# One set of activation tiles, overwritten in halves, for all stages of the first two blocks of a hybrid decoder step

## The chip, the cores and the metric

The kernel runs on one core of one Trainium2 chip. The metric is the device time of one execution in microseconds. TensorE does the matmuls, VectorE and ScalarE the elementwise work, GpSimd (POOL in the profile) a part of it, and SyncE (SP) issues the DMAs. Each engine works through its own queue in order.

## What is computed

One decoder layer over a prompt of 2048 tokens and 8 x 8 sample tokens, width 1024, in float32:

```python
mix = jnp.concatenate([oa, ob, oc, od], axis=-1).astype(dt) @ prm['w_out'][li]
h = h + mix

gu = rmsnorm(h, prm['norm2_g'][li]) @ prm['w_ffn_in'][li]
h = h + (jax.nn.silu(gu[..., :D_FF]) * gu[..., D_FF:]) @ prm['w_ffn_out'][li]

gate = jax.nn.sigmoid(rmsnorm(h, prm['ple_norm_g'][li]) @ prm['w_ple_gate'][li])
h = h + (pl @ prm['w_ple'][li]) * gate
```

Ahead of that stands an RMSNorm, a projection `w_in` and four token mixers (a to d), whose outputs are `oa` to `od`; behind it a last RMSNorm gives `y_prompt`. D_FF is 2816.

## The kernel before

The prompt is cut into four blocks of 512 tokens, each of four row tiles of 128 tokens. First `in_proj` runs for all blocks (to about 885 us); then, for each block, the part after the mixers: `rest(0)`, `rest(1)`, `rest(2)`, and `rest7(3)` for the last block with the sample rows. The mixers of a block run between and beside these stages: `mixers(b)` and `rest(b)` are written one after the other, and a scheduler orders all instructions by priority (`S.at(...)`, the table `PRIO`) and by when it expects operands to be ready. `S.at(0)` puts an instruction ahead of everything that is ready.

Matmuls of float32 are made of three passes: every operand is split into a high part, cast by ScalarE (`split` line 306, scaled 309, weights line 290), and a low part, the difference, on VectorE (307, 310) or for half of the weights on GpSimd (293). An activation tile `act` holds 128 of the 1024 features for all 512 tokens, high and low; `act8` (line 231) takes eight of them from a pool of eight in the stages after the mixers. The passes are hi x hi, hi x lo, lo x hi.

`rest` (line 511) works so. `mixed` (line 646) loads the four mixer outputs, 128 x 1024 each (line 657), and splits them into eight act tiles. Four residual tiles `h` of 128 x 1024 are loaded from x_prompt (`load_x`, line 388, DMA issue at line 391) into a pool of five buffers. `out_mm` (line 444) multiplies by w_out: four columns of 256, and in each column four row tiles; one row tile and column is 24 matmuls into one PSUM bank (`mm_a`, matmuls at line 374), and `add` (line 520) adds it to `h`. The matmuls of blocks 0 and 1 share three PSUM banks; from `rest(2)` on there are six.

The second norm needs all of a row of `h`. `Norm.prep` takes the reciprocal root (`rstd`, lines 323 to 335) and scales the rows into an `xs` tile (line 68); `Norm.step` transposes one feature tile of two row tiles on TensorE (line 85) and splits it into an act tile. With one pool of act tiles the norm's tiles come from the same eight buffers as those of the output projection, so its steps are written after all of w_out. Only block 2 has a second pool (`act2`) and hands the norm to `out_mm`, which calls `prep` and `step` as soon as row tiles have their last column.

Then the feed-forward part (`mm_b`, matmuls at line 354; w_ffn_out again through `out_mm` with columns of 512), the ple norm, and `per_layer_out`: four quarters of gate (w_ple_gate, 24 matmuls) and up (w_ple, 6 matmuls) for every row tile, lines 592 to 594. After the last quarter `finish(i)` (line 578) scales row tile i and stores it to y_prompt (line 579); the `h` buffer is free when the store has read it.

Here and in the prediction C is the boundary of blocks 0 and 1, B the second norm of block 0 and D that of block 1. A line after the change is the line before plus 1 near line 85 to 510, and plus 2 or 1 in `rest`: 307 is 308, 374 is 375, 391 is 392, 520 is 522, 578 is 579.

Of the kernel before, what the change touches and what calls it, by code (L numbers as in the profile page):

```python
# [11 lines left out]
F32 = mybir.dt.float32  # L12
# [9 lines left out]
D = 1024  # L22
T = 2048
TB = 512
NB = T // TB
NS = 64
TBS = TB + NS
# [9 lines left out]
class Norm:  # L37
# [1 line left out]

    def __init__(self, S, src, gain, groups, scale=True, ahead=True):
        self.S, self.src, self.gain, self.groups, self.scale, self.ahead = S, src, gain, groups, scale, ahead
        self.acts, self.rows, self.ready, self.r = S.act8(TBS if (4,) in groups else TB), {}, {}, {}
        self.last, self.done, self.fresh = groups[-1][-1], set(), True
        self.of = {i: g[-1] for g in groups for i in g}
        self.it = self.steps()
        if ahead:
            with S.at(0):
                self.rows = {i: src(i) for i in [i for g in groups for i in g][:4]}  # L50
# [142 lines left out]
class Step:  # L193
# [314 lines left out]
            self.split(pas[k], ps[:, k * NS:(k + 1) * NS])  # L508
        return pa, pas

    def rest(self, b, mix, smix):

        nc, I, O = self.nc, self.I, self.O
        with_s = smix is not None
        tiles = [i for i, _ in self.tiles(with_s)]
        h = {}

        def add(i, c, ps):
            d = h[i][:, c]
            nc.vector.tensor_tensor(d, ps, d, op=ALU.add)  # L520

        acts = self.mixed(mix, smix)
        nt = TBS if with_s else TB
        for i in tiles:
            h[i] = self.load_x(self.hp.tile([128, D], F32, name="h"), b, i)
        norm2 = lambda **k: self.norm(lambda i: (h[i], False), self.gain["norm2_g"], with_s, **k)

        norm = norm2(ahead=False) if len(self.actps) > 1 else None
        self.out_mm(acts, I["w_out"][0], KT, 256, with_s, add, norm)
        norm = norm or norm2()  # L530
        wi, wo = I["w_ffn_in"][0], I["w_ffn_out"][0]
        KC = 3
        f0 = 0
        while f0 < FT:
            n = KC if f0 else FT % KC
            gs = []
            if f0 + n == FT:
                pa, pas = self.per_layer(b, with_s)
            for f in range(f0, f0 + n):
                us = [self.units([wi[:, c0:c0 + 128]], KT, 4) for c0 in (f * 128, D_FF + f * 128)]  # L540
                if f:
                    ps = [self.mm_b(u, acts, KT, with_s) for u in us]
                else:

                    acts, w0 = norm.upto(1), TB // 2
                    t = self.bank()
                    ps = [[(0, w0, self.mm_piece(t[:, j * w0:(j + 1) * w0], u, acts, KT, 0))] for j, u in enumerate(us)]
                    norm.all()
                    for p, u in zip(ps, us):
                        t = self.bank()[:, :nt - w0]  # L550
                        p.append((w0, nt - w0, self.mm_piece(t, u, acts, KT, w0)))
                g = self.gp.tile([128, 2, TBS], F32R, name="g", tag="g")
                gs.append(g)
                for (t, m, gate), (_, _, up) in zip(*ps):
                    th = self.ev.tile([128, TBS], F32, name="ev")[:, :m]
                    nc.scalar.activation(th, gate, AF.Tanh, scale=0.5)
                    nc.vector.scalar_tensor_tensor(th, th, 1.0, gate, op0=ALU.add, op1=ALU.mult)
                    nc.vector.scalar_tensor_tensor(th, th, 0.5, up, op0=ALU.mult, op1=ALU.mult)
                    self.split(g[:, :, t:t + m], th)
            w = wo[f0 * 128:(f0 + n) * 128]  # L560
            f0 += n
            if f0 < FT:
                self.out_mm(gs, w, n, 512, with_s, add)
        norm = self.norm(lambda i: (h[i], False), self.gain["ple_norm_g"], with_s, scale=False, ahead=False)
        self.out_mm(gs, w, n, 512, with_s, add, norm, True)
        self.per_layer_out(b, h, norm, pa, pas)

# [75 lines left out]
                self.out_mm(*last, 512, with_s, add, norm, True, mid=with_s)  # L643
                self.per_layer_out(b, h, norm, pa, pas)

    def mixed(self, mix, smix):

        nc = self.nc
        with_s = smix is not None
        acts = self.act8(TBS if with_s else TB)  # L650
        if with_s:
            ms = self.ev.tile([128, TBS], F32, name="ev")[:, :KT * NS].rearrange("p (k n) -> p k n", k=KT)
# [2 lines left out]
        for j in range(4):  # L655
            m = self.xsp.tile([128, D], F32, name="xs").rearrange("p (k n) -> p k n", k=2)
# [1421 lines left out]
def step_kernel(ctx, tc, I, O):  # L2078
    nc = tc.nc
    S = Step(ctx, nc, tc, I, O)  # L2080
# [10 lines left out]
    mix = [m for _, m in zm]  # L2091
# [35 lines left out]
    with S.working("p", 16):  # L2127
        norm = S.in_proj(0, z[0], None, S.norm1(0, False), (1, True))
# [3 lines left out]
        norm = S.in_proj(2, z[2], None, norm, (3, False))  # L2132
        mixers(1)
        S.in_proj(3, z[3], None, norm)
    with S.working("f", 8, 3, 5):
        S.rest(0, mix[0], None)
        mixers(2)
        S.rest(1, mix[1], None)
        mixers(3)
        M.banks.close()  # L2140
        sample_mixers()
        with S.tc.tile_pool(name="act2", bufs=KT, reuse_waits="tile") as p:
            S.actps, S.nacts = [p] + S.actps, 0
            with S.more():
                S.rest(2, mix[2], None)
# [21 lines left out]
```

## Time and profile before

| | before |
|---|---|
| median of 3 runs | 3416.94 us (3409.40 to 3417.16) |
| the profiled execution | 3413.59 us, span 3411.8 us |
| TensorE busy | 3304.8 us, 97% of the span |
| TensorE weight loads | 82% |
| VectorE, ScalarE, GpSimd busy | 61%, 39%, 22% |
| mean granted TensorE clock | 0.982 |

Times are microseconds from the start of the span. A row of a timeline is: start, duration, engine and line, operation, output <- inputs, shape, how many; in brackets the idle time of the engine ahead of it and what ended it. SPq rows are the issues of DMAs on SyncE's queue. Matmuls overlap in the pipeline, so a row's duration is longer than the distance to the next.

### The profile page before, as it was taken

To read this page: it belongs to the slowest core of one execution; us is meant where nothing else is said; L and a number is where in the kernel's file an instruction comes from. 1 tells how busy PE (TensorE), PEld (TensorE's weight loads), DVE (VectorE), ACT (ScalarE), POOL (GpSimd) and SP (SyncE) were. 2 spreads that over 40 slices of the span, in tenths; PEclk is the share of its full clock that TensorE was granted. 3 is DMA by queue.
4 is the path that set the end of the run, shared out by engine and by line. 5 is a ranking of instruction groups with operands and counts; after the bars stand their busy time and mean duration, and the time that the engine had idled before them with its cause. 6 is when DMAs were issued, how large, how long until landed. Compare 5 with 4: busy or idle time off the path is not lost. (4 is left out here: it accounts for less than half of the span.)

```text
span 3411.8 us, 64337 instructions
## 1 busy us (share of the span) xinstructions
PE 3304.8 (97%) x23998; PEld 2784.0 (82%) x23998; DVE 2067.0 (61%) x5691; ACT 1322.2 (39%) x2753; POOL 756.4 (22%) x656
## 2 busy tenths in 40 slices
PE   7999999999999999998999999999999999999998
PEld 6788987878887778788878777788777789889888
DVE  4455566654577756588876457754332466877765
ACT  4433445323344223355333335344233244434343
POOL 2212112122112122112112212131121222334321
PEclk9999999999999999999999999999999999999999
DMA  7645445544433333444333443344544543223222
GB/s 211 185 121 146 128 119 157 153 126 146 128 106 104 98 91 112 116 115 129 114 98 105 121 113 106 108 137 135 148 138 121 156 145 121 63 81 93 77 89 69
DMA packets 621756, 411.78 MB, mean 121 GB/s; under 512 B 155357, under 2 KB 572876, under 8 KB 621444
## 3 DMA queue, kind: packets, MB, share of 16 engines
q1 hardware_dynamic: 618184, 405.12, 41.1%
q8 instruction: 189, 3.10, 0.4%
q10 hardware_dynamic: 3260, 2.55, 0.3%
q14 instruction: 123, 1.01, 0.1%
HBM read 348.77 MB, written 61.18 MB: 120 GB/s over the span
## 5 line engine op out<-in xcount | busy, mean ns | idle before, releaser
L354 PE MATMUL mmp<-act,whi 128*128 128x512 f32 (+1 forms) x3616 | 1108.0, 386 | 6.6 <-ACT ev L378 4.3
L293 POOL TENSOR_TENSOR wlo<-wraw,whi 128x512 fp32r<-128x512 f32 (+1 forms) x400 | 557.9, 1397 | 2055.0 <-ACT whi L290 1314.6
L290 ACT CAST whi<-wraw 128x512 fp32r<-128x512 f32 (+1 forms) x800 | 491.6, 619 | 840.1 <-PE mmp L354 342.3
L354 PEld LDWEIGHTS mmp<-act,whi 128*128 128x128 f32 x3616 | 657.6, 190 | 137.2 <-ACT ev L378 5.4
L354 PE MATMUL mmp<-act,wlo 128*128 128x512 f32 (+1 forms) x1808 | 687.4, 386 | 0.0
L374 PE MATMUL mmp<-whi,act 128*128 128x256 f32 (+3 forms) x2992 | 572.6, 289 | 14.8 <-DVE act L307 6.8
L293 DVE TENSOR_TENSOR wlo<-wraw,whi 128x512 fp32r<-128x512 f32 (+1 forms) x400 | 314.6, 787 | 312.9 <-ACT whi L290 282.7
L374 PE MATMUL mmp<-whi,g 128*128 128x512 f32 (+1 forms) x1496 | 485.8, 402 | 8.5 <-DVE xs L743 4.3
L374 PEld LDWEIGHTS mmp<-whi,act 128*128 128x128 f32 (+1 forms) x2992 | 470.2, 190 | 25.5 <-DVE act L307 7.4
L374 PE MATMUL mmp<-wlo,act 128*128 128x256 f32 (+2 forms) x1496 | 430.4, 289 | 2.5 <-DVE wlo L293 2.4
L354 PEld LDWEIGHTS mmp<-act,wlo 128*128 128x128 f32 x1808 | 339.1, 189 | 64.2 <-issue 2.5
L374 PEld LDWEIGHTS mmp<-whi,g 128*128 128x128 f32 (+1 forms) x1496 | 271.3, 186 | 77.8 <-DVE xs L743 6.9
L374 PE MATMUL mmp<-wlo,g 128*128 128x512 f32 (+1 forms) x748 | 296.3, 397 | 0.0
L374 PEld LDWEIGHTS mmp<-wlo,act 128*128 128x128 f32 (+1 forms) x1496 | 282.9, 189 | 8.3 <-issue 3.3
L520 DVE TENSOR_TENSOR h<-mmp,h 128x512 f32<-128x512 f32 (+1 forms) x240 | 149.9, 633 | 111.7 <-PE mmp L374 100.5
L374 PEld LDWEIGHTS mmp<-wlo,g 128*128 128x128 f32 (+1 forms) x748 | 138.8, 186 | 33.2 <-issue 0.2
L762 PE MATMUL mmp<-Sb,whi 128*128 128x288 f32 x800 | 161.8, 296 | 0.9 <-DVE xs L743 0.5
L739 POOL TENSOR_TENSOR wlo<-wraw,whi 128x512 fp32r<-128x512 f32 x80 | 112.5, 1410 | 195.3 <-ACT whi L738 188.0
L762 PEld LDWEIGHTS mmp<-Sb,whi 128*128 128x128 f32 x800 | 129.2, 188 | 4.3 <-DVE xs L743 2.6
L1690 ACT ACTIVATE b_sb<-b_sb,b_nm 128x256 f32<-128x256 f32 (+5 forms) x128 | 66.9, 523 | 136.5 <-DVE b_nm L1689 122.6
L762 PE MATMUL mmp<-Sb,wlo 128*128 128x288 f32 x400 | 117.9, 296 | 0.0
L310 DVE SCALAR_TENSOR_TENSOR act<-mmp,gcol,act 128x256 fp32r<-128x256 f32 (+1 forms) x192 | 85.3, 460 | 46.5 <-ACT act L309 45.7
(472 smaller groups left out, 4723.3 us busy)
## 6 DMA issues: line engine op xcount, KB each, us to landing
wraw<-w_ffn_in SPq DMA_DIRECT2D x352, 256.0 KB
wraw<-w_in SPq DMA_DIRECT2D x208, 256.0 KB
wraw<-w_ffn_out SPq DMA_DIRECT2D x176, 256.0 KB
wraw<-w_out SPq DMA_DIRECT2D x64, 256.0 KB
wraw<-w_ple_gate SPq DMA_DIRECT2D x64, 256.0 KB
bs_K<-cache_b_k SPq DMA_DIRECT2D x48, 256.0 KB
xs<-x_prompt SPq DMA_DIRECT2D x16, 512.0 KB
h<-x_prompt SPq DMA_DIRECT2D x16, 512.0 KB
```

Source lines behind the costliest of these rows:

```text
L290: nc.scalar.copy(hi, raw)
L293: eng.tensor_tensor(lo, raw, hi.bitcast(F32), op=ALU.subtract)
L310: nc.vector.scalar_tensor_tensor(lo, src, scale, hi.bitcast(F32), op0=ALU.mult, op1=ALU.subtract)
L354: nc.tensor.matmul(ps, u[a], acts[k][:, b, t:t + w], start=i == 0, stop=i == n)
L374: nc.tensor.matmul(ps, acts[k][:, b, t0:t0 + rows], units[k][a], start=i == 0, stop=i == n)
L520: nc.vector.tensor_tensor(d, ps, d, op=ALU.add)
L739: eng.tensor_tensor(lo, x, hi.bitcast(F32), op=ALU.subtract)
L762: nc.tensor.matmul(ps, w[a][:, k], op[k][:, b], start=first and k == 0 and j == 0, stop=k == 3 and j == 2, skip_group_check=True)
L1690: nc.scalar.activation(sb, sb, AF.Exp, bias=nm, accum_out=l)
```

## The change

`rest(0)` and `rest(1)` get one set of eight act tiles, `acts`, allocated once ahead of both. With it:

- `mixed` loads each mixer output in two halves of 256 tokens, eight DMAs of 128 x 2 x 256 into four `xs` tiles in place of four DMAs of 128 x 1024, and splits each half into its half of the act tile: per block 16 casts and 16 low parts of 256 columns in place of 8 and 8 of 512.
- The second norm is made ahead of `out_mm` and handed to it, and writes into the same tiles (`acts=place`): the halves of the tokens that w_out's last column has read are overwritten while the other half is still being read. The ple norm writes into them too.
- The pool of residual tiles has four buffers in place of five.

The program has 20044 matmuls before and after.

```diff
-    def __init__(self, S, src, gain, groups, scale=True, ahead=True):
+    def __init__(self, S, src, gain, groups, scale=True, ahead=True, acts=None):
...
-        self.acts, self.rows, self.ready, self.r = S.act8(TBS if (4,) in groups else TB), {}, {}, {}
+        self.acts = acts or S.act8(TBS if (4,) in groups else TB)
+        self.rows, self.ready, self.r = {}, {}, {}
...
-    def rest(self, b, mix, smix):
+    def rest(self, b, mix, smix, acts=None):
...
-        acts = self.mixed(mix, smix)
+        place, acts = acts, self.mixed(mix, smix, acts)
...
-        norm = norm2(ahead=False) if len(self.actps) > 1 else None
+        norm = norm2(ahead=False, acts=place)
         self.out_mm(acts, I["w_out"][0], KT, 256, with_s, add, norm)
-        norm = norm or norm2()
...
-        norm = self.norm(lambda i: (h[i], False), self.gain["ple_norm_g"], with_s, scale=False, ahead=False)
+        norm = self.norm(lambda i: (h[i], False), self.gain["ple_norm_g"], with_s, scale=False, ahead=False,
+                         acts=place)
...
-    def mixed(self, mix, smix):
+    def mixed(self, mix, smix, place=None):
...
+        if place:
+            w = TB // 2
+            for t in (0, w):
+                for j in (0, 2):
+                    m = self.xsp.tile([128, D], F32, name="xs").rearrange("p (j k n) -> p j k n", j=2, k=2)
+                    for i in range(2):
+                        nc.sync.dma_start(out=m[:, i], in_=mix[j + i][:, :, t:t + w])
+                    for k in range(4):
+                        self.split(place[2 * j + k][:, :, t:t + w], m[:, k // 2, k % 2])
+            return place
...
-    with S.working("f", 8, 3, 5):
-        S.rest(0, mix[0], None)
+    with S.working("f", 8, 3, 4):
+        acts = S.act8(TB)
+        S.rest(0, mix[0], None, acts)
         mixers(2)
-        S.rest(1, mix[1], None)
+        S.rest(1, mix[1], None, acts)
```

What it does to the order of the instructions, at the places that the prediction speaks of:

SyncE's queue at C, before. `y_prompt<-h` are the stores of block 0's row tiles, `h<-x_prompt` the loads of residual rows (the first row tile of block 1 was loaded much earlier), `xs<-mix_c` and `xs<-mix_d` two of the loads of block 1's mixer outputs.

```order
L579 DMA y_prompt<-h 128x1024
L391 DMA h<-x_prompt 128x1024
L579 DMA y_prompt<-h 128x1024
L657 DMA xs<-mix_c 128x1024
L657 DMA xs<-mix_d 128x1024
L288 DMA wraw<-w_out 128x2x256
L391 DMA h<-x_prompt 128x1024
L288 DMA wraw<-w_out 128x2x256 x7
L579 DMA y_prompt<-h 128x1024
L288 DMA wraw<-w_out 128x2x256
L391 DMA h<-x_prompt 128x1024
L579 DMA y_prompt<-h 128x1024
```

The same place in the changed program, from the last of the eight half loads of mixer outputs.

```order
L657 DMA xs<-mix_d 128x2x256
L580 DMA y_prompt<-h 128x1024
L392 DMA h<-x_prompt 128x1024
L289 DMA wraw<-w_out 128x2x256 x5
L580 DMA y_prompt<-h 128x1024
L392 DMA h<-x_prompt 128x1024
L289 DMA wraw<-w_out 128x2x256 x3
L580 DMA y_prompt<-h 128x1024
L289 DMA wraw<-w_out 128x2x256
L392 DMA h<-x_prompt 128x1024
L580 DMA y_prompt<-h 128x1024
L392 DMA h<-x_prompt 128x1024
```

All loads of mixer outputs moved ahead of the first store, and each of the four residual loads now follows a store of block 0; before, three followed one and the fourth store was followed by block 2's first.

VectorE at C, before, from the first adds of block 1's row tiles 1 and 2. L520 are the adds, L578 is block 0's finish, here of row tile 2, L293 the low halves of weights; L9xx are mixer d, L13xx mixer c, L33x the reciprocal root.

```order
L520 TENSOR_TENSOR h<-mmp,h 128x256 x2
L334 SCALAR_TENSOR_TENSOR ss<-ss 128x1
L1359 TENSOR_TENSOR c_X<-c_X,c_tmp 128x24x2
L335 SCALAR_TENSOR_TENSOR ss<-ss 128x1
L293 TENSOR_TENSOR wlo<-wraw,whi 128x512
L335 SCALAR_TENSOR_TENSOR ss<-ss 128x1
L1357 TENSOR_TENSOR c_tmp<-c_x,c_X 128x69
L970 SCALAR_TENSOR_TENSOR d_g<-d_a,d_g 128x1024
L334 SCALAR_TENSOR_TENSOR ss<-ss 128x1
L578 SCALAR_TENSOR_TENSOR h<-h,ss,fg 128x1024
```

VectorE in the changed program, from the finish of row tile 2 (the add that stands here is the first one of row tile 1).

```order
L982 SCALAR_TENSOR_TENSOR d_i<-d_i,d_g 128x1024
L579 SCALAR_TENSOR_TENSOR h<-h,ss,fg 128x1024
L294 TENSOR_TENSOR wlo<-wraw,whi 128x512
L1368 TENSOR_TENSOR c_tmp<-c_x,c_X 128x54
L336 SCALAR_TENSOR_TENSOR ss<-ss 128x1
L522 TENSOR_TENSOR h<-mmp,h 128x256
L1370 TENSOR_TENSOR c_X<-c_X,c_tmp 128x9x6
L335 SCALAR_TENSOR_TENSOR ss<-ss 128x1
L1368 TENSOR_TENSOR c_tmp<-c_x,c_X 128x48
L336 SCALAR_TENSOR_TENSOR ss<-ss 128x1
L1370 TENSOR_TENSOR c_X<-c_X,c_tmp 128x8x6
L579 SCALAR_TENSOR_TENSOR h<-h,ss,fg 128x1024
```

Before, three adds of block 1 stood ahead of the finish of row tile 2; now one does, and the first add of row tile 1 stands between the finishes of row tiles 2 and 3.

TensorE at B, before: L374 is the last matmul of w_out, L85 the norm's transposes, the others mixers.

```order
L374 MATMUL mmp<-whi,act 128x256
L1833 MATMUL mx<-ident,b_a1r 128x128
L1806 MATMUL mx<-b_kT,b_qc 32x64 x3
L1559 MATMUL mx<-c_S,c_kg 64x64 x4
L1806 MATMUL mx<-b_kT,b_qc 32x64
L1811 MATMUL mx<-b_kT,b_qc 128x128 x2
L85 MATMUL mmp<-ident,xs 128x128 x2
```

TensorE at B in the changed program: the norm's transposes are L86; the first stand twelve rows further up, behind row tile 2 of w_out's last column; the L375 rows are row tile 3 of that column.

```order
L86 MATMUL mmp<-ident,xs 128x128 x2
L1711 MATMUL mx<-ident,b_sb 128x128 x2
L1711 MATMUL mx<-ident,b_sb 64x128
L86 MATMUL mmp<-ident,xs 128x128 x2
L1586 MATMUL acc<-c_y,c_S 64x64 x2
L1570 MATMUL mx<-c_S,c_kg 64x64 x4
L1586 MATMUL acc<-c_y,c_S 64x64 x2
L375 MATMUL mmp<-whi,act 128x256 x2
L375 MATMUL mmp<-wlo,act 128x256
```

The transposes of row tiles 0 and 1 moved from behind the whole of w_out to between its last two tiles.

## Rows read from the trace of the kernel before

**Rows 1.** The page's first part: busy time and share of each engine.

```profile
PE 3304.8 (97%) x23998; PEld 2784.0 (82%) x23998; DVE 2067.0 (61%) x5691; ACT 1322.2 (39%) x2753; POOL 756.4 (22%) x656
```

**Rows 2.** Waits of TensorE: engine, line, releaser: us in total, times, longest.

```profile
PE mmp L374 <- DVE h L520: 7.3, 7, 2.2
PE mmp L374 <- DVE act L307: 6.8, 3, 5.3
```

**Rows 3.** Windows: busy us of each engine, granted clock, DMA share, GB/s.

```profile
957.00:975.00 18.00, 15.37 (x137) 12.48 (x136) 16.31 (x76) 11.92 (x28) 5.10 (x5) 0.82 0.44 130
1588.30:1600.00 11.70, 6.38 (x31) 6.17 (x30) 11.70 (x23) 10.23 (x20) 5.81 (x3) 0.71 0.88 306
...
1640.00:1685.00 45.00, 40.51 (x491) 35.65 (x490) 38.75 (x120) 20.28 (x42) 8.19 (x9) 0.89 0.37 98
2300.00:2345.00 45.00, 44.54 (x416) 39.21 (x414) 21.81 (x68) 21.75 (x38) 8.99 (x9) 1.00 0.48 141
```

**Rows 4.** Timeline of TensorE at C.

```profile
1593.95 0.58 PE L374 MATMUL mmp<-whi,act 128*128 128x256 f32 x1 [5.32 <-DVE act L307]
...
1604.74 0.38 PE L374 MATMUL mmp<-whi,act 128*128 128x256 f32 x1 [1.16 <-DVE act L307]
...
1607.47 0.50 PE L374 MATMUL mmp<-whi,act 128*128 128x256 f32 x2 [0.69 <-DVE h L520]
...
1618.49 0.51 PE L374 MATMUL mmp<-whi,act 128*128 128x256 f32 x2 [2.22 <-DVE h L520]
...
1623.16 0.49 PE L374 MATMUL mmp<-whi,act 128*128 128x256 f32 x2
```

**Rows 5.** Timeline of VectorE at C: finishes, first low halves, one add.

```profile
1587.04 1.27 DVE L578 SCALAR_TENSOR_TENSOR h<-h,ss,fg 128x1024 f32<-128x1024 f32 x1
...
1593.21 1.88 DVE L307 TENSOR_TENSOR act<-xs,act 128x512 fp32r<-128x512 f32 x3
...
1613.76 2.40 DVE L578 SCALAR_TENSOR_TENSOR h<-h,ss,fg 128x1024 f32<-128x1024 f32 x1
...
1619.35 1.28 DVE L578 SCALAR_TENSOR_TENSOR h<-h,ss,fg 128x1024 f32<-128x1024 f32 x1
...
1624.54 0.42 DVE L520 TENSOR_TENSOR h<-mmp,h 128x256 f32<-128x256 f32 x1 [2.31 <-DMA h<-x_prompt]
```

**Rows 6.** Timeline of SyncE's queue at C, and one load at the start of block 2.

```profile
1583.38 0.42 SPq L579 DMA_DIRECT2D y_prompt<-h  x1
1586.67 0.36 SPq L391 DMA_DIRECT2D h<-x_prompt  x1
1588.34 0.34 SPq L579 DMA_DIRECT2D y_prompt<-h  x1
...
1592.96 0.33 SPq L391 DMA_DIRECT2D h<-x_prompt  x1
...
1619.62 0.34 SPq L391 DMA_DIRECT2D h<-x_prompt  x1
1620.65 0.74 SPq L579 DMA_DIRECT2D y_prompt<-h  x1
1625.72 0.33 SPq L391 DMA_DIRECT2D h<-x_prompt  x1
...
2275.64 0.34 SPq L391 DMA_DIRECT2D h<-x_prompt  x1
```

**Rows 7.** Timeline of VectorE at the start of block 2: the add behind that load.

```profile
2281.98 0.42 DVE L520 TENSOR_TENSOR h<-mmp,h 128x256 f32<-128x256 f32 x1 [2.40 <-DMA h<-x_prompt]
```

**Rows 8.** Timeline of TensorE: end of w_out and transposes at B, D and block 2.

```profile
961.93 0.28 PE L374 MATMUL mmp<-whi,act 128*128 128x256 f32 x1
...
964.04 0.44 PE L85 MATMUL mmp<-ident,xs 128*128 128x128 f32 x2
...
967.15 0.44 PE L85 MATMUL mmp<-ident,xs 128*128 128x128 f32 x2 [0.80 <-DVE xs L68]
...
1659.68 1.70 PE L1182 MATMUL mx<-a_q,a_k 64*64 64x32 f32 x28 [1.61 <-DVE a_k L1206]
...
2336.33 0.41 PE L85 MATMUL mmp<-ident,xs 128*128 128x128 f32 x2 [0.29 <-DVE act L310]
```

## The prediction

> **What bounds the kernel now.** The profile's page comes first: TensorE is busy for 3304.8 of 3411.8 us [rows 1], so at most about 107 us of its span is not matmul, and the changed program issues the same matmuls. A gain can only come from TensorE's idle time and from its time at half clock. The waits of TensorE come second: in the output projection (line 374) it waits 7.3 us for the residual adds (line 520) and 6.8 us for the low halves of the activations (line 307) [rows 2]. Windows come third: the places that the diff touches are block 0's second norm (957 to 975), the start of block 1 (1588 to 1629), block 1's second norm (1640 to 1685) and the start of block 2. TensorE's idle share and the granted clock of each stand in [rows 3]. Then the timelines, for the wait that ends last at each place.
>
> The profiled run took 3413.6 us, 3.3 us below the median of the three runs (3416.9). The sum is made against 3413.6, and 3.3 us is added at the end. A measurement of this kernel can tell about 0.3% from no change, which is 10.3 us.
>
> **Start of block 1, which I call C.** Time counts from 1588.3, where the last gate matmul of block 0 is issued. TensorE then idles 5.32 us until the first low halves are there, and again 1.16, 0.69 and 2.22 us [rows 4], and the window 1588.3 to 1600 has a mean clock of 0.71, part of it at 1.2 GHz in place of 2.4: 0.29 of 11.7 us lost, 3.4 us [rows 3]. The 5.32 us end when VectorE reaches its first low halves at 1593.21 [rows 5]; two of the four loads of mixer outputs stood behind a store and a load of residual rows that wait [rows 6], as the order of the queue shows. **Removed:** in the changed order all eight half loads stand ahead of the first y_prompt store, and the first token half is split before the last gate tiles. The ceiling is the four gaps and the clock, 9.4 + 3.4 = 12.8 us.
>
> **Added:** 8 more loads on SP's queue, which stand ahead of the stores, where no matmul waits on them. 16 more low splits on VectorE, half as long: three of 512 columns took 1.88 us, 0.63 each [rows 5]; a 256-column VectorE instruction takes 0.42 [rows 5]. For one block that is 16 x 0.42 - 8 x 0.63 = 1.7 us, on an engine that has not a pause in 1588.3 to 1600 [rows 3], so it counts: inside the adds' dates below.
>
> **The new wait.** With four residual buffers, tile i of block 1 can be loaded only when tile i of block 0 is scaled by finish (line 578), stored, and landed; before, tile 0 was loaded early and tiles 1, 2, 3 followed stores 0, 1, 2. What one round takes: store to next load 3.3, 4.6 and 5.1 us (1583.38 to 1586.67, 1588.34 to 1592.96, 1620.65 to 1625.72), load to add 4.9 us (1619.62 to 1624.54) [rows 5, 6] and 6.3 us (2275.64 to 2281.98) [rows 6, 7]. Sum: 8 to 11.4 us. A sentence apart: the Trainium skill (DMA: Bandwidth & Descriptors, Anatomy of one DMA) fits 2.0 us plus bytes over 436 GB/s, which for two transfers of 512 KB is 6.4 us; by it the third tile's add would come 1.6 to 5 us earlier and C would cost about 1 us instead of my 5. The rows here show longer, so I go by the rows.
>
> When do the finishes come? I walked VectorE's rows in the changed order from the last gate tile on, each at the duration its line has in the trace: from finish(0) to finish(1) 46 instructions, among them eight low halves, three 1024-column multiplies and two scans; to finish(2) 24 more, to finish(3) 10. finish(0) ends about 0, finish(1) about +16, finish(2) about +23.5, finish(3) about +26.5 us (before: -5, 0, +27.8 and +32.3, from [rows 5] and the first store in [rows 6]). Then: the add of tile 0 at +8 to +11; the matmuls of tiles 1 to 3 of the first column wait for it, because only three PSUM banks serve these matmuls, and run to about +18. Behind them TensorE's queue has eight row sums of the d mixer, whose input comes off VectorE and ScalarE at about +24: some 6 us idle. Tile 1's add comes at about +24.7 and releases the second column. Its tile 1 waits for the add of tile 2: +23.5 + 8 to 11.4 = +31.5 to +35, a second idle stretch of 4 to 7 us. A tile is 24 matmuls; three tiles ran from 1607.47 to 1616.27 (1618.49 less the gap of 2.22) [rows 4], 2.9 us each. Two tiles later the second column's tile 3 starts at +37 to +41. Before it starts at 1623.16, +34.9 [rows 4]. So C is 2 to 6 us **slower**, and two idle stretches of over 4 us can bring half clock as the 5.32 us gap did: another 1 to 3. I take **+5**; ends -12.8 (no h wait binds) and +12 (each round at its longest, both stretches followed by half clock).
>
> **Second norm of block 0, B.** Before, TensorE does all of w_out first, to 962.2, and the transposes after it: the first at 964.04, a gap of 0.80 ahead of a later one [rows 8]. The clock is 0.82 in 957 to 975, 3.2 us lost, and 2.6 us are idle (18 - 15.37) [rows 3]. The first transposes wait for the rows scaled by line 68, which hang on VectorE, not on TensorE. In the changed order these transposes stand ahead of the last tile of w_out's last column, so TensorE, in order, comes to them 2.9 us sooner, at about 959.3, and stops to 964.0 but for some mixer matmuls: 4.4 us. That tile's 2.9 us of matmuls later fill the 2.6 us of gaps, and about 0.8 of the clock's loss may come back: 4.4 - 2.6 - 0.8 = **+1**; ends -5.8 (2.6 idle and 3.2 of clock all gone) and +4.
>
> **Second norm of block 1, D.** Idle 4.5 of 45 us, clock 0.89, 5.0 us lost [rows 3]; a gap of 1.61 us stands for them [rows 8]. The same interleaving, but here mixer a's chunks stand between and also wait for VectorE, which is 86% busy [rows 3]. The nearest row for a gain is block 2, which already makes its norm inside w_out: 0.29 us idle there and full clock [rows 3, 8], though with six banks, two activation sets and a VectorE 48% busy. I take a third of the 9.5: **-3**; ends -9.5 and +4.
>
> **The rest.** Start of block 2: its tile 0 is no longer loaded early, yet six banks serve there and no matmul waited though VectorE waited 2.40 us for a load [rows 7]: **+1**, ends 0 and +4. Block 0's start has no residual to wait for and its loads stand at the same place: 0, ends -1 and +2. The ple norm in place writes columns that the last feed-forward part has read long before: 0; its cover is w_ffn_out's eight tiles, and without them the first gate tile would wait for the transposes' splits as [rows 8] show it, some 2 us. The scheduler also reorders the mixers everywhere from 885 us to 2780 us, where I found no wait with a sign: 0, ends -5 and +5.
>
> **Sum:** +5 + 1 - 3 + 1 = +4, so 3417.6 for the profiled run and, with 3.3, **3421 us** against the median. That is +0.1%: no change that can be measured.
>
> **Rivals.** The forecast itself, with a net of a few microseconds either way from C, B and D, has a chance of 0.28. *Faster, the early loads pay.* The activation waits go and the adds find their rows: -12.8 at C and -8 at D and B, about -20, so **3397**. For: [rows 2] has just these waits, and block 2 shows the norm hidden [rows 8]. Against: finish(2) and finish(3) still come behind 20 us of VectorE work. It needs a round of store and load under 5 us. A sentence apart: the Trainium skill's shorter fit for a DMA goes this way, but by its 6.4 us C only comes to about +1. Chance 0.27.
>
> *Slower, four buffers and three banks.* TensorE is in order, so each late add stops everything behind it, mixers too. If the round takes 11.4 us for tiles 2 and 3, and half clock follows two stretches, C is +12 and B +4, D 0, block 2 +2: +18, **3435**. It decides where the add of tile 2 comes later than +35, since then the whole second column is late. A rule speaks for it, in the Trainium skill (Trainium Kernel Development and Optimization, Best Practices): double-buffer, so that DMA overlaps compute; taking away the buffer that loaded ahead undoes that, and the trace agrees as far as VectorE's 2.31 us wait for a load goes [rows 5]. Chance 0.31.
>
> *The change does nothing here*, because the act tiles were never the last thing waited for: the waits at C move from activations to adds and D's from scaled rows to the same scaled rows, within 3 us, **3417**. Against: the orders differ at all three places. Chance 0.14; it is within 0.3% too.
>
> **Chances and range.** Within 0.3% (3406.7 to 3427.2): 0.28 + 0.14 = 0.42; faster: 0.27; slower: 0.31. Adding the ends of every term gives -34 and +31, but they don't fall together. The range takes the two rivals' times and leaves about one in ten beyond each: 3394 to 3438. The likeliest case's own range is 3409 to 3429.
>
> **What would show it.** At C, no wait of line 375 for line 308 (right on the removal), but waits of it for line 522, with idle stretches ahead of the row sums and ahead of the second column's tile 1 totalling over 9 us. h loads issued 3.3 to 5.1 us behind their stores. At B one stop of 3 to 5 us ahead of a transpose. If instead the adds find their rows and TensorE idles under 3 us in C, the forecast is wrong on the fast side; if the time moves by over 10 us with C, B and D as forecast, it is wrong because of the reordering elsewhere.

## The result and the profile after

| | before | after |
|---|---|---|
| median | 3416.54 us (3409.40 to 3417.16, 4 runs) | 3457.76 us (3455.91 to 3461.72, 4 runs) |
| ratio to before | | 1.0124, 95% interval 1.0106 to 1.0143 |
| the profiled execution's span | 3411.8 us | 3454.1 us |
| mean granted TensorE clock | 0.982 | 0.970 |

The change made the kernel 1.24% slower, some 41 us. The forecast was 3421 us with a range that ended at 3438. The sign of its +4 came out right by luck: the forecast itself called +4 no change that can be measured, and what moved the time is a term that it had put at 0.

The page of the changed kernel, first its busy times, then TensorE's clock in 40 slices of the span:

```profile
PE 3329.2 (96%) x23998; PEld 2804.3 (81%) x23998; DVE 2081.2 (60%) x5707; ACT 1320.8 (38%) x2769; POOL 746.6 (22%) x656
...
PEclk9999999999999999989899999999999999999999
```

Against [rows 1]: the same 23998 matmul records take 24.4 us longer (3329.2 against 3304.8), and TensorE is idle 18 us longer (3454.1 - 3329.2 = 124.9, before 107.0). So over half of the 42 us between the two spans is not waiting: the same matmuls take longer. The time in which TensorE is busy at half clock, 1.2 GHz, rose from 105 to 175 us (the recorded clock laid beside its busy time); the slices below 9 run from 1468 to 1554 and from 1641 to 1727 us.

TensorE's waits in the changed kernel (engine, line, releaser: us in total, times, longest), to be held against [rows 2]:

```profile
PE mx L996 <- ACT d_r L990: 9.0, 2, 7.8
PE mmp L86 <- DVE act L311: 7.7, 12, 1.3
PE mmp L355 <- DVE h L522: 6.2, 2, 4.1
...
PE mmp L86 <- DVE ev L594: 3.7, 4, 2.0
...
PE mmp L375 <- DVE h L522: 2.5, 2, 1.8
...
PE mmp L375 <- DVE act L308: 0.3, 1, 0.3
```

The wait that the change set out to remove is gone: 6.8 us of line 307 became 0.3 of line 308. The waits of the output projection for the adds did not grow either (7.3 to 2.5 us), though the feed-forward part now waits 6.2 us for adds. What grew is the wait for mixer d's row sums, to 9.0 us, and that of transposes for the ple gate's work on VectorE, to 3.7 us. The kernel before had there:

```profile
PE mx L985 <- ACT d_r L979: 1.3, 1, 1.3
...
PE mmp L85 <- DVE ev L593: 0.6, 2, 0.4
```

Windows of the kernel before at the places concerned (columns as in [rows 3]: window, length, busy us of TensorE, weight loads, VectorE, ScalarE, GpSimd, then clock, DMA share, GB/s):

```profile
945.00:1025.00 80.00, 77.31 (x736) 64.99 (x735) 58.96 (x217) 37.74 (x92) 12.56 (x11) 0.96 0.41 111
1425.00:1460.00 35.00, 32.77 (x244) 25.44 (x243) 19.68 (x47) 14.91 (x33) 9.98 (x10) 0.99 0.68 181
1500.00:1550.00 50.00, 48.59 (x446) 43.80 (x446) 40.82 (x160) 24.72 (x59) 4.47 (x5) 0.97 0.29 79
1580.00:1632.00 52.00, 41.78 (x308) 39.52 (x306) 46.45 (x127) 27.77 (x49) 13.19 (x8) 0.93 0.51 166
1640.00:1700.00 60.00, 55.51 (x629) 47.79 (x628) 50.27 (x153) 24.87 (x51) 11.06 (x11) 0.91 0.34 92
...
1985.00:2015.00 30.00, 30.00 (x203) 23.47 (x202) 15.31 (x51) 11.13 (x24) 6.86 (x6) 1.00 0.41 120
```

And of the changed kernel, at the same places of the program:

```profile
945.00:1030.00 85.00, 77.35 (x705) 65.19 (x705) 65.76 (x235) 39.73 (x96) 12.46 (x11) 0.90 0.36 100
1425.00:1460.00 35.00, 29.57 (x292) 21.86 (x283) 20.08 (x65) 14.69 (x36) 8.57 (x9) 0.76 0.59 164
1508.00:1560.00 52.00, 42.76 (x333) 37.04 (x332) 39.13 (x143) 23.15 (x56) 6.94 (x5) 0.84 0.33 100
1594.00:1664.00 70.00, 56.38 (x377) 53.05 (x378) 57.43 (x171) 33.26 (x68) 14.85 (x12) 0.83 0.41 132
1664.00:1740.00 76.00, 69.28 (x782) 59.87 (x782) 52.16 (x165) 26.69 (x55) 10.39 (x10) 0.87 0.34 97
2025.00:2055.00 30.00, 30.00 (x220) 21.37 (x221) 13.02 (x45) 9.57 (x23) 4.64 (x5) 0.72 0.48 107
```

Two numbers tell a place's loss: the idle time (length less TensorE's busy time) and the clock's (length times one less PEclk). They overlap where TensorE idles at half clock, and the windows do not hold exactly the same mixer work, so they rank the places and don't add up to the 41 us. Block 0's second norm, B: 7.7 idle and 8.5 by the clock, before 2.7 and 3.2. Near 1440 us: 5.4 and 8.4, before 2.2 and 0.4. Block 0's ple norm: 9.2 and 8.3, before 1.4 and 1.5. The boundary C: 13.6 and 11.9, before 10.2 and 3.6. D: 6.7 and 9.9, before 4.5 and 5.4. Near 2040 us nothing is idle at all, and 8.4 us go by the clock; the same matmuls of the feed-forward part start near 1988 us in the kernel before, at full clock. At three of these six places (1440, 1530 and 2040) the prediction has no term other than 0.

The place near 1440 us, timeline of TensorE in the changed kernel:

```profile
1437.30 1.09 PE L1080 MATMUL mx<-ident,c_y 128*128 128x128 f32 x4 [1.47 <-DVE c_y L1538]
1440.43 1.09 PE L1080 MATMUL mx<-ident,c_y 128*128 128x128 f32 x4 [1.42 <-DVE c_kd L1090]
1442.90 0.48 PE L1844 MATMUL mx<-ident,b_a1r 128*128 128x128 f32 x1 [1.38 <-DVE b_a1r L1874]
```

These are mixers c and b of block 2 alone, each step waiting for VectorE, with no large matmul between; the clock falls to half at 1434.8, ahead of the first of these waits, and stays there for 17.1 us. In the kernel before, matmuls of the feed-forward part stand between the same mixers, the two gaps of this stretch end in such matmuls, and the clock is 0.99:

```profile
1436.84 0.73 PE L354 MATMUL mmp<-act,whi 128*128 128x512 f32 x2 [1.39 <-ACT whi L290]
1438.41 0.74 PE L354 MATMUL mmp<-act,whi 128*128 128x512 f32 x2 [0.84 <-ACT whi L290]
```

Block 0's ple norm, same view; the last group of transposes before the second half of the gate tiles:

```profile
1527.46 0.44 PE L86 MATMUL mmp<-ident,h 128*128 128x128 f32 x2 [1.26 <-DVE ev L594]
1529.92 0.44 PE L86 MATMUL mmp<-ident,h 128*128 128x128 f32 x2 [2.02 <-DVE ev L594]
...
1536.40 0.79 PE L375 MATMUL mmp<-whi,act 128*128 128x256 f32 x2 [1.69 <-DVE act L311]
```

Between the two halves of the transposes stand two row tiles of gate and up matmuls in both kernels. Counted in the timelines, 106 mixer matmuls stand among them in the kernel before, and none in the changed one.

The boundary C, same view:

```profile
1622.87 0.80 PE L375 MATMUL mmp<-whi,act 128*128 128x256 f32 x2 [1.82 <-DVE h L522]
1640.79 3.58 PE L996 MATMUL mx<-ones,d_r 128*128 128x1 f32 x16 [7.76 <-ACT d_r L990]
```

and SyncE's queue there, two of the four rounds of store and load:

```profile
1630.75 0.36 SPq L580 DMA_DIRECT2D y_prompt<-h  x1
1633.41 0.34 SPq L392 DMA_DIRECT2D h<-x_prompt  x1
...
1640.87 0.36 SPq L580 DMA_DIRECT2D y_prompt<-h  x1
...
1644.59 0.34 SPq L392 DMA_DIRECT2D h<-x_prompt  x1
```

The first idle stretch came as worked out (7.76 us ahead of the row sums; some 6 were expected), the second, ahead of the second column's tile 1, did not. VectorE there, a window and three rows of its timeline: block 0's finishes of row tiles 1 and 2 and block 1's first add of row tile 1:

```profile
1625.00:1643.70 18.70, 10.94 (x78) 10.73 (x77) 18.70 (x47) 5.85 (x9) 5.67 (x4) 0.77 0.40 141
```

```profile
1629.45 1.27 DVE L579 SCALAR_TENSOR_TENSOR h<-h,ss,fg 128x1024 f32<-128x1024 f32 x1
...
1639.57 1.27 DVE L579 SCALAR_TENSOR_TENSOR h<-h,ss,fg 128x1024 f32<-128x1024 f32 x1
...
1641.56 0.41 DVE L522 TENSOR_TENSOR h<-mmp,h 128x256 f32<-128x256 f32 x1
```

VectorE has no pause in these 18.7 us, and the add, 8.2 us behind the issue of its load (1633.41), did not wait for it.

### The profile page after: what moved, and what is told of

Read it like the earlier page. It is cut to its first block, busy times and chain, and to the rows that moved or that the text cites. A ratio compares the mean times of both kernels' runs of the same rounds, so it can differ in the third digit from the quotient of the medians.

```text
span 3454.1 us, 64338 instructions
## 1 busy us (share of the span) xinstructions
PE 3329.2 (96%) x23998; PEld 2804.3 (81%) x23998; DVE 2081.2 (60%) x5707; ACT 1320.8 (38%) x2769; POOL 746.6 (22%) x656
## 4 chain that ended last, share of the span: by engine, by line
PE 79%; DVE 10%; DMA 5%; SPq 3%; issue 2%; ACT 1%; POOL 0%; DVEq 0%; ACTq 0%; POOLq 0%
PE mmp L355 31%; PE mmp L375 26%; PE mmp L773 4%; SPq L1379 2%; PE acc L1910 1%; DMA wraw<-w_ffn_in 1%; PE mmp L364 1%; PE mx L1711 1%; PE mx L1765 1%; DVE wlo L294 1%; PE mmp L86 1%; PE mx L1193 1%; PE mx L1822 1%; PE mmp L733 1%; PE mx L1972 1%
## 5 line engine op out<-in xcount | busy, mean ns | idle before, releaser
L294 POOL TENSOR_TENSOR wlo<-wraw,whi 128x512 fp32r<-128x512 f32 (+1 forms) x400 | 545.7, 1366 | 2093.1 <-ACT whi L291 1458.5
L375 PE MATMUL mmp<-whi,act 128*128 128x256 f32 (+3 forms) x2992 | 578.2, 291 | 9.1 <-DVE act L311 3.1
L375 PEld LDWEIGHTS mmp<-whi,act 128*128 128x128 f32 (+1 forms) x2992 | 476.5, 193 | 19.9 <-issue 5.5
L375 PE MATMUL mmp<-whi,g 128*128 128x512 f32 (+1 forms) x1496 | 486.8, 403 | 5.0 <-DVE xs L754 3.3
L375 PE MATMUL mmp<-wlo,act 128*128 128x256 f32 (+2 forms) x1496 | 433.9, 291 | 4.8 <-DVE wlo L294 4.8
L375 PEld LDWEIGHTS mmp<-whi,g 128*128 128x128 f32 (+1 forms) x1496 | 273.2, 187 | 74.8 <-DVE xs L754 5.9
L375 PE MATMUL mmp<-wlo,g 128*128 128x512 f32 (+1 forms) x748 | 298.4, 400 | 0.0
L375 PEld LDWEIGHTS mmp<-wlo,act 128*128 128x128 f32 (+1 forms) x1496 | 286.6, 192 | 9.4 <-DVE wlo L294 5.7
L375 PEld LDWEIGHTS mmp<-wlo,g 128*128 128x128 f32 (+1 forms) x748 | 139.9, 187 | 33.4 <-issue 0.2
```

The source lines that it names most:

```text
L294: eng.tensor_tensor(lo, raw, hi.bitcast(F32), op=ALU.subtract)
L375: nc.tensor.matmul(ps, acts[k][:, b, t0:t0 + rows], units[k][a], start=i == 0, stop=i == n)
```

## The experiments

Three theories stood after the result, named by letters that have nothing to do with the places B, C and D. Theory A is the prediction's own, the four buffers; theory C is the norm inside w_out by itself. Theory B: the change moves the mixers' work in the order, by itself and not by its waits. The mixers get fixed priorities from the table `PRIO = [20000,201600,204600,205600,206907]`, while the instructions of `rest` are numbered as they are written. The change writes 4 more DMAs and 16 more splits into each block, so from block 0's feed-forward part on every instruction of `rest` has a number higher by 20, by 40 in block 1, and the table was made for the old numbers. Counting up to the start of block 0's feed-forward part gives 204078 before and 204098 after. Theory B comes in two forms: B1, the table no longer fits the numbering, so that a table shifted along with it gives the time back; B2, any edit lays the mixers anew, and since the table was searched for the old program, another order tends to be slower. Putting the set of tiles in place alone, with full-width loads, five buffers and the norm after w_out, leaves TensorE's order row for row as before, so that part was not run.

Ratios are to the kernel before, runs on the same chip, with their 95% intervals; three rounds each.

**Parts of the change.** *h5*: all of the change, five buffers.

```diff
-    with S.working("f", 8, 3, 4):
+    with S.working("f", 8, 3, 5):
```

> The changed kernel with five residual buffers in place of four; all else as changed. Theory A (the fifth buffer: with four, row tile i of block 1 waits for the store of row tile i of block 0, and the adds come late): the loss at the boundary of blocks 0 and 1 (22.7 us idle or at half clock, 13.2 before) goes, and what follows from it: about 3430 to 3440 us. Theory B (the order of the mixers' work changed and lies badly beside the norms; the buffer is a small part): 3448 to 3462 us, the loss around 1430 to 1545 us stays. Theory C (norm inside w_out costs by itself): as B.

3463.9 us, 1.0133 (1.0111 to 1.0156): no faster than with four. TensorE's timeline at place C shows what holds the second column now:

```profile
1639.34 0.80 PE L375 MATMUL mmp<-whi,act 128*128 128x256 f32 x2 [5.84 <-DVE h L522]
```

The adds are late with the fifth buffer too. Theory A falls as the cause of the 41 us.

*before_h4*: the kernel before with `S.working("f", 8, 3, 4)`.

> The kernel before with four residual buffers in place of five. Theory A: the boundary of blocks 0 and 1 gets 5 to 20 us slower, 3422 to 3437 us. Theory B: within 5 us of before unless the order of the mixers moves too.

3425.1 us, 1.0016 (1.0003 to 1.0029). The buffer costs 0.16%, 0.29% at the end of the interval; the order differs from before only from place C on.

*halves_only*: the change with five buffers, and the norm as before.

```diff
-        norm = norm2(ahead=False, acts=place)
+        norm = norm2(ahead=False) if len(self.actps) > 1 else None
         self.out_mm(acts, I["w_out"][0], KT, 256, with_s, add, norm)
+        norm = norm or norm2(acts=place)
```

> One set of act tiles, mixer outputs loaded and split in halves, second norm after w_out as before, five residual buffers. Theory A: the first low halves come early, the 5.3 us wait at the boundary is gone, and nothing takes its place: 3405 to 3412 us. Theory B: slower than before by the mixers' order, 3430 us or more, with loss around 1430 to 1545 us. Theory C: as A.

3433.1 us, 1.0044 (1.0030 to 1.0059): slower, as theory B said and theories A and C did not.

*norm_only*: the norm inside w_out, loads at full width (`mixed` takes `acts = place or self.act8(...)` and has no halves), five buffers.

> One set of act tiles, second norm inside w_out's last column, but mixer outputs loaded and split at full width, five residual buffers. Theory A: near 3417 us, since the buffer is there. Theory C (transposes ahead of the last tile stop TensorE, which is in order): +4 us at the second norms of both blocks each, some 3425 us or more. Theory B: anything, by how the scheduler happens to lay the mixers; losses then also lie where neither norm nor loads are.

3439.7 us, 1.0065 (1.0050 to 1.0080). Here no instruction is added, so the table fits, and it is slower all the same. That is above the 3425 us of theory C, but it does not show that the norm costs by itself: from block 0's second norm on, the order of the mixers on TensorE differs from before here too.

**The table alone.** *before_m20* is the kernel before with the table 20 lower, *before_p20* 20 higher:

```diff
-PRIO = [20000,201600,204600,205600,206907]
+PRIO = [20000,201600,204580,205580,206887]
```

> The kernel before with the table moved by -20 (204580, 205580, 206887), which puts the mixers to the feed-forward part of block 0 as the change does, and nothing else. Theories B1 and B2: slower by 5 to 35 us with no edit of loads, norms or buffers, with more time at half clock between 880 and 2800 us than the 68 us of before. Theory C: within 5 us of before.

> The kernel before with the table moved by +20 (204620, 205620, 206927), nothing else. Theory B1 (the old table is right for the old numbering and any shift costs): slower by 5 to 25 us, 3425 to 3445 us. Theory B2 (each table lays the mixers anew, with a spread of some 20 us): anything between 3405 and 3445 us. Theory C (the order is of no account): within 5 us of before.

20 lower: 3438.5 us, 1.0060 (1.0037 to 1.0083). 20 higher: 3423.1 us, 0.9999 (0.9983 to 1.0015). A shift of twenty numbers, with no load, norm, split or buffer touched, costs half of what the change cost; twenty the other way cost nothing, against the 5 to 25 us of B1. The timeline of TensorE in before_m20 has the three waits of the changed kernel at the same place:

```profile
1436.97 0.76 PE L1069 MATMUL mx<-ident,c_y 128*128 128x128 f32 x4 [1.47 <-DVE c_y L1527]
...
1441.77 1.09 PE L1069 MATMUL mx<-ident,c_y 128*128 128x128 f32 x4 [3.42 <-DVE c_kd L1079]
...
1444.24 0.48 PE L1833 MATMUL mx<-ident,b_a1r 128*128 128x128 f32 x1 [1.38 <-DVE b_a1r L1863]
```

and the window of that place the same clock:

```profile
1425.00:1460.00 35.00, 28.62 (x232) 20.84 (x230) 20.11 (x61) 14.15 (x35) 8.61 (x9) 0.76 0.57 157
```

*table_p20* and *table_p40* are the changed kernel with the table moved along by 20 (204620, 205620, 206927) and by 40.

> The changed kernel with the table PRIO moved by +20 for the mixers of blocks 2 and 3 and the samples (204620, 205620, 206927): the change writes 20 more numbered instructions into each block ahead of its feed-forward part, so with this the mixers stand to block 0's feed-forward part as before. Theory B1 (the table no longer fits the numbering): most of the 41 us is gone, 3417 to 3430 us. Theory B2 (any edit lays the mixers anew, and this table was searched for the old program): the time moves by ten or more us in either direction, but not surely back, 3425 to 3470 us. Theory C (the change's own waits): 3450 to 3460 us.

> The changed kernel with the table moved by +40 (204640, 205640, 206947), which fits the numbering of block 1 (40 more numbers by then) and is 20 too far for block 0. Theory B1: near the changed kernel with +20, 3430 to 3440 us, or a little worse. Theory B2: anything between 3415 and 3465 us.

3435.5 us, 1.0047 (1.0031 to 1.0062), and 3435.7 us, 1.0039 (1.0023 to 1.0055). Moving the table takes back 26 of the 41 us. That is below B1's forecast, which was most of the 41, and table_p40 does no better than table_p20. The same window in table_p20, with the three waits gone:

```profile
1425.00:1460.00 35.00, 31.77 (x221) 24.51 (x222) 17.42 (x42) 9.22 (x21) 8.18 (x9) 0.95 0.47 114
```

Two signs go together over all runs: half clock for 17 us or more on end from between 1433 and 1440 us, and block 0's ple norm without mixers between its halves. The changed kernel, h5 and only0 have none there and before_m20 has 4; the same four with a table 20 higher have 67 to 106, and no run outside these four has under 37, or more than 6.8 us on end at half clock between 1400 and 1480 us. But halves_only, with the same 20 numbers and the old table, shows neither sign (52 mixer matmuls): a misfit does not always bring them.

**By block.** *only0* and *only1* give `acts` to one of the two calls of `rest` and keep the norm after w_out in the other block, four buffers; *only0_p20* is only0 with the table at +20; *only1_h5* is only1 with five buffers. The texts call the change's own local waits theory C here.

> The change for block 0 alone (block 1 keeps its own tiles, full-width loads, norm after w_out; four residual buffers). If the loss is made of local waits (theory C): what lies before 1580 us in the changed kernel stays, some 25 us over before, and the boundary and block 1 are as before: about 3440 us. Theory B: the loss moves with the order; also places that this edit does not touch differ.

> The change for block 1 alone. Theory C: the time to 1580 us as before, the boundary and block 1's norm as in the changed kernel, about +15 us: 3432 us. Theory B: the time to 1580 us is near before, since the numbering changes only from block 1 on; after it anything between 3410 and 3450 us.

> The change for block 0 alone with the table moved by +20. With the old table block 0 alone costs +1.42% and block 1 alone +0.13%. If the table's fit to block 0's numbering is the cause of nearly all of that: within 0.5% of before, 3420 to 3437 us, and the pattern of three waits near 1440 us with some 17 us of half clock behind it is not there. If the norm in block 0's w_out itself is what costs: still 3455 us or more.

> The change for block 1 alone with five residual buffers. Theory A (adds of block 1 wait for stores of block 0): 5 us or more faster than block 1 alone with four, 3415 to 3420 us. If VectorE's queue, not the store, holds the adds: within 4 us of it, 3421 to 3429 us.

only0: 3466.3 us, 1.0142 (1.0111 to 1.0173). only1: 3425.2 us, 1.0013 (1.0000 to 1.0026). only0_p20: 3440.6 us, 1.0062 (1.0047 to 1.0078). only1_h5: 3430.0 us, 1.0021 (1.0008 to 1.0034). The whole loss comes with block 0, whose numbering the mixers of block 2 run beside, and more than half of it goes with the table. Local waits alone had given some 3440 us for only0, which came out 26 us over that, and 3432 for only1, which came out 7 under. The expectation for only0_p20 was within 0.5%; it missed that by 0.12.

**What is left.** *halves_p20* and *halves_p40* are halves_only with the moved table, *h5_p20* is h5 with it, *norm1_p20* is halves_p20 with the norm inside w_out for block 1, *norm0* the norm inside w_out for block 0 and nothing else, old table; *halves1* the halves for block 1 alone, five buffers, old table.

> Halves of the mixer outputs in place, norm after w_out, five buffers, table moved by +20 (with the old table +0.44%). If the misfit of the table is its whole cost: 3410 to 3424 us. If the halves cost by themselves: 3430 us or more.

> As halves_p20 with the table at +40, which fits the numbering of block 1 and is 20 too far for block 0: 3410 to 3425 us if a table that is too late does no harm (as +20 did none to the kernel before), 3430 us or more if any misfit does.

> The changed kernel with the table moved by +20 and five residual buffers. If the fourth of a percent or so that is left after the table is the wait of residual loads for stores: near before, 3418 to 3427 us. If it is VectorE's queue at the boundary and the norm inside w_out: as with four, 3430 to 3442 us.

> Halves for both blocks, norm inside w_out for block 1 alone, table +20, five buffers: the candidate that leaves out what cost most, the norm inside block 0's w_out. If block 0's norm is all that is left of the loss: as halves_p20, 3412 to 3424 us; a version better than both kernels would be under 3408. If the norm inside w_out costs in block 1 too: 3430 us or more.

> The norm inside w_out for block 0 alone, full-width loads, five buffers, old table (no instruction is added, so the numbering fits). By my prediction's step B +1 us; by block 0 alone with the fitted table (+0.62%) and the norm in both (+0.65%): +12 to +20 us, 3432 to 3441 us, with a loss at 955 to 1010 us.

> For block 1 alone: halves of the mixer outputs in place, norm after w_out as before, five residual buffers. What the removed waits are worth by themselves: by my sum of the boundary 12.8 us at most, so 3407 us if nothing takes their place; 3415 to 3425 us if VectorE's queue then holds the adds.

| kernel | us | ratio | interval |
|---|---|---|---|
| halves_p20 | 3419.9 | 0.9991 | 0.9976 to 1.0007 |
| halves_p40 | 3435.5 | 1.0041 | 1.0024 to 1.0057 |
| h5_p20 | 3438.0 | 1.0054 | 1.0038 to 1.0071 |
| norm1_p20 | 3422.7 | 1.0009 | 0.9996 to 1.0022 |
| norm0 | 3430.4 | 1.0021 | 1.0007 to 1.0036 |
| halves1 | 3432.5 | 1.0028 | 1.0018 to 1.0039 |

The halves with a table that fits cost nothing and gain nothing. Adding the norm to block 1 moves that by 0.18%, within the intervals; adding it to both makes 0.63%, so block 0's norm is the larger part there, some 0.45%. Alone (norm0) it measured 0.21%, some 7 us where 12 to 20 were expected, and with full-width loads the shares lie the other way round: norm_only less norm0 leaves 0.44% for block 1's norm. The costs of the two norms don't add up one by one; what each costs hangs on the order around it. The buffers are nothing here either (h5_p20 against table_p20). halves_p40 speaks against a simple rule: a table 20 too late for block 0 cost 0.5% there, though 20 too late cost the kernel before nothing. halves1, whose numbers change only from block 1 on, missed both of its expectations (3407, and 3415 to 3425); its cause stays open. So the record decides between B1 and B2 only in part: +20 gave time back in all four pairs, as B1 said, but a table that fits is neither always needed nor always enough. That no kernel was faster than the one before, clear of noise, agrees with B2, which no run tests by itself.

Why the halves gain nothing shows at place C in halves_p20, timeline of TensorE:

```profile
1616.44 0.51 PE L375 MATMUL mmp<-whi,act 128*128 128x256 f32 x2 [3.90 <-DVE h L522]
```

This one wait for an add stands where [rows 4] has 5.32, 1.16, 0.69 and 2.22 us: 5.5 us of the 9.4 are gained. Then, before that block's second norm:

```profile
1655.00:1680.00 25.00, 18.32 (x154) 15.71 (x155) 19.78 (x71) 11.07 (x22) 6.19 (x6) 0.66 0.44 119
```

6.7 us idle and a clock of 0.66, 8.5 us, in a place that the halves don't touch; [rows 3] has 4.5 and 5.0 us in the 45 us about it. That this takes back the gain is read from the trace, not tested.

## Why the prediction was wrong, step by step

- **The step that failed** is one sentence in "The rest": "The scheduler also reorders the mixers everywhere from 885 us to 2780 us, where I found no wait with a sign: 0, ends -5 and +5." Runs with the table alone moved show a term of +20 us (before_m20), and of 18 to 27 us, by the ratios, in the four pairs with and without +20 on edited kernels (table_p20, only0_p20, h5_p20, halves_p20). The evidence was there: the table of priorities and the added instructions are both in the code, and the prediction's own last sign names the reordering elsewhere. Looking for a wait with a sign was the wrong search. What the traces show in its place is mixers that moved from between large matmuls into stretches of their own: alone near 1440 us, each step waiting for VectorE at half clock, and missing at block 0's ple norm, where they had filled the wait.
- **The half clock was put only beside idle gaps.** The prediction gave it 1 to 3 us at C. 24.4 of the 42 us are matmuls that take longer, and near 2040 us the clock is 0.72 with no idle time at all.
- **The ple norm at 0** was wrong by place: 9.2 us idle and a clock of 0.84 near 1530 us. The prediction named w_ffn_out's eight tiles as the cover; what had covered the second half of the transposes was the 106 mixer matmuls between the halves, and they are gone. table_p20 has 67 there and doesn't have these waits. It goes with the table.
- **B, +1**, was too small. The stop ahead of the first transposes is there, 1.77 us and not 4.4, but behind it the clock is half for 10 us and the feed-forward part waits for an add:

```profile
960.76 0.80 PE L86 MATMUL mmp<-ident,xs 128*128 128x128 f32 x3 [1.77 <-DVE xs L69]
...
1021.09 0.74 PE L355 MATMUL mmp<-act,whi 128*128 128x512 f32 x2 [4.12 <-DVE h L522]
```

  The norm inside block 0's w_out is worth 7 us alone (norm0) to 15 us (h5_p20 less norm1_p20). The same waits, at much the same times, stand in table_p20 and only0_p20; halves_p20 has neither. How much of them is the interleaving and how much the order it leads to stays open.
- **C, +5, ends -12.8 and +12**: 13.6 us idle against 10.2 and a lower clock, within the ends. The reason was half right. The activation waits went, and the row sums' stall came. The round of store and load, on which the sum rested, is not what TensorE waited for: row tile 1's add did not wait for its load, and row tile 2's, which did for 2.28 us, held no matmul; loads followed stores by 2.7 to 5.1 us. What came late is VectorE's queue. With finish(0) at 0, the next three finishes ended at 18.6, 28.7 and 31.6 us; the prediction's walk had 16, 23.5 and 26.5. No run tests that queue by itself. By the Trainium skill (DMA: Bandwidth & Descriptors, Anatomy of one DMA) a round would take 6.4 us, an estimate from a fit that the section gives for DMAs issued by GpSimd, while SyncE issues these. No run here times a round by itself.
- **D, -3**, did not come (6.7 us idle against 4.5, and a lower clock); block 1 alone (only1) has a net of +0.13%, with everything at C in it. **Start of block 2, +1**: before_h4 shows 0.16%, up to 0.29% by its interval, for both places of the buffer together.
- **The rival "slower, four buffers and three banks"** named the right side for a wrong reason; its rule on double buffering (the Trainium skill, Trainium Kernel Development and Optimization, Best Practices) is borne out by no run here, for the pairs with four and five buffers differ by no more than 0.1%, and before_h4 from before by 0.16%.

## What to carry to other kernels

Where a scheduler orders instructions against a table of fixed priorities, adding instructions moves everything after them against that table: shift the table with the numbering, and time a shifted table on the old kernel, before judging the edit itself. A gain at one wait is worth little if the rest of the order is not held still; here a shift of 20 numbers cost 20 us in one direction and nothing in the other, and the longest wait of TensorE in the kernel before is 10.3 us. Shifting the table gave back 26 of the 41 us, not all. Ask of every wait that an edit moves which other matmuls had filled it, and read the granted clock of stretches in which small matmuls run alone, not only the idle gaps.

## What the runs showed of the hardware

The clock fell with no idle gap ahead. Near 2040 us the changed kernel's TensorE was busy for all of 30 us, and the granted clock fell to half, 1.2 GHz, at 2032.2 for 17.1 us. TensorE's timeline there:

```profile
2028.38 0.40 PE L355 MATMUL mmp<-act,wlo 128*128 128x512 f32 x1
...
2029.30 0.38 PE L1228 MATMUL acc<-a_at,a_v 64*64 64x64 f32 x5
...
2031.20 0.86 PE L1255 MATMUL acc<-a_q,a_Ss 64*64 64x8 f32 x22
...
2034.47 1.39 PE L1255 MATMUL acc<-a_q,a_Ss 64*64 64x8 f32 x22
...
2045.26 1.22 PE L355 MATMUL mmp<-act,whi 128*128 128x512 f32 x2
```

From 2028.7 to 2045.3 us mixers alone are on the engine; the same 22 of them take 0.86 us before the fall and 1.39 after. A busy share of 100% in a row is thus no sign of 2.4 GHz; the PEclk column has to be read beside it.

VectorE's smallest instructions become long beside GpSimd when they read two SBUF inputs. In the changed kernel one-column instructions of VectorE took 0.17 us on average where no GpSimd instruction overlapped (733 of them, none over 0.8 us), and 0.47 where one did (87, of which 26 over 0.8 us). All 26 are of the 50 with two inputs (TENSOR_TENSOR, SCALAR_TENSOR_TENSOR), 0.70 us on average; the 37 beside GpSimd with one input took 0.16 us, none over 0.21. VectorE and GpSimd at place C:

```profile
1635.40 1.23 DVE L336 SCALAR_TENSOR_TENSOR ss<-ss 128x1 f32<-128x1 f32 x1
...
1641.49 0.15 DVE L336 SCALAR_TENSOR_TENSOR ss<-ss 128x1 f32<-128x1 f32 x1
```

```profile
1635.23 2.66 POOL L294 TENSOR_TENSOR wlo<-wraw,whi 128x512 fp32r<-128x512 f32 x2 [3.60 <-ACT whi L291]
```

The same instruction takes 0.15 us, or 1.23 beside the low halves of weights on GpSimd. The Trainium skill (GPSIMD Engine Reference, Specifications) says that GpSimd's SBUF interfaces are shared with VectorE and names two cases of contention, a 2-port mode of VectorE and instructions with two SBUF inputs; the rows agree on the second case and give its price; the first none of them shows. VectorE's median durations, with which the prediction dated the adds, leave this out: between finish(1) and finish(2) three such instructions took 1.00, 1.23 and 1.21 us in place of 0.15 to 0.21, 2.9 us more, and that stretch came out 2.6 us longer than the walk had it (10.1 against 7.5).
